# Four reorderings in a two-layer trunk: columns in a shared PSUM bank, three outputs of the layer norm first, ten weight lows on VectorE, four outputs at a time

## The chip, the core and the metric

The kernel runs on one core of a Trainium2 chip. The metric is the device time of that core in microseconds (us). The engines are TensorE (PE in the profile), VectorE (DVE), ScalarE (ACT), GpSimd (POOL) and SyncE (SP). SyncE and GpSimd issue the transfers from HBM (DMA).

## What is computed

A trunk of two layers over 1024 tokens of 1024 channels, all in float32. Each layer has a token mixer and a SwiGLU FFN, each behind an RMS norm and shifted, scaled and gated by a modulation vector. In layer 0 the mixer is a convolution module, in layer 1 a pooling mixer.

```python
def conformer_conv(h, w1, b1, w_dw, b_dw, ln_g, ln_b, w2, b2):
    u = h @ w1 + b1
    a, g = jnp.split(u, 2, axis=-1)
    u = a * jax.nn.sigmoid(g)
    u = lax.conv_general_dilated(u, w_dw[:, None, :], ...) + b_dw   # depthwise, causal, width 31
    u = jax.nn.silu(layer_norm(u, ln_g, ln_b))
    return u @ w2 + b2

def reference(x, c, ...):
    c_act = jax.nn.silu(c)
    for i in range(DEPTH):
        mod = c_act @ ada_w[i] + ada_b[i]
        sh_m, sc_m, g_m, sh_f, sc_f, g_f = jnp.split(mod, N_ADA, axis=-1)
        h = modulate(rms_norm(x, norm_mix_g[i]), sh_m, sc_m)
        y = conformer_conv(h, ...) if i % 2 == 0 else multiscale_pool(h, ...)
        x = x + (1.0 + g_m)[:, None, :] * y
        h = modulate(rms_norm(x, norm_ffn_g[i]), sh_f, sc_f)
        y = (jax.nn.silu(h @ w_gate) * (h @ w_up)) @ w_down
        x = x + (1.0 + g_f)[:, None, :] * y
    return rms_norm(x, final_g)
```

`multiscale_pool` takes trailing means over 2, 4, 8 and 16 tokens in four groups of channels, and then a linear map for each group. The FFN has 2816 inner columns, 22 tiles of 128.

## The kernel before

**Tiles.** The channels lie on the 128 partitions in eight tiles, the tokens in two chunks, A and B, of 512 columns. Nearly all products are 128x512: a weight tile of 128x128, 512 tokens moving. To keep float32 precision every operand is split into a high and a low half, and a product is three matmuls (high by high, high by low, low by high: `products`, L420). A unit of work is mostly one weight tile row of 128x1024, which makes 8 products, 24 matmuls.

**Weights.** `load_weight` (L406 to L418) fetches a weight as `raw` with SyncE, ScalarE rounds it to the high half (a CAST), and the low half comes about in one of two ways. By default, ScalarE writes the rounded negative of the weight into the low tile and GpSimd issues a transfer that adds the weight from HBM onto it (L414): that takes ScalarE a second pass, a place in GpSimd's queue and a second fetch. With `low` given, that engine subtracts the high half from `raw` in one operation. There are nine units of buffer (`W_BUFS`), of which a weight costs two halves, so that few weights are held ahead. `run_units` (L541 to L572) goes through the list of units in order. After each unit and at each weight taken it starts the load of the next weight as long as the held ones fit.

**Order.** TensorE's order is the order in which the program is written; VectorE, ScalarE and GpSimd get the operations as units and tasks emit them, with a running estimate of the engines' clocks that decides where a task takes its next step and which engine does a flexible operation (`either`). Instructions on an engine run in their order, so whatever waits holds what is behind it. Operations of these engines all have the line of the helper, L108; matmuls have L130.

**Convolution stage.** For each tile `p`, TensorE makes `a` and `g`, ScalarE the sigmoid `t<-g` and VectorE the product `u`. The 31 taps are split: VectorE adds its part into `ca`, ScalarE multiplies (`pr`) and GpSimd adds (`pa`); VectorE joins them (`ca<-pa,ca`), makes `u` and adds it to `acc`. The layer norm (`layer_norm_silu`, L777 to L812) starts with the product `mean` of `acc`, then `var` and `rstd`, and then for each of eight tiles SiLU, `vhi` and `vlo`. `conv_out` (L814 to L838) makes the outputs `y`; its first unit makes outputs 0 and 1 together, tile by tile of the layer norm, the others one by one. It is called for A right after the convolution stage, and for B near the end of A's FFN of layer 0.

**Modulation.** `ada_columns` (L360 to L385) runs beside it: `ada` sums for one of the four remaining vectors, loads of two tiles (`adaw`) at a time; ScalarE copies the rows; `columns_done` (L389 to L399) turns the rows into columns by four small matmuls into `adac`, and VectorE adds the bias into `mod`, from which GpSimd makes the `gains`. PSUM has six banks for `mm` tiles, which are handed out in turn: `ada`, `adac`, `a`, `g`, `y`, `gate`, `up` and `dn` all take from them, and a new tile waits for the readers of the old tile in its bank.

**FFN.** `ffn_p1` (L907) makes `gate` and `up` of one inner tile, then `t`, `ghi`, `glo`; `ffn_p2` (L932 to L942) makes the eight outputs `dn` of two or more inner tiles, and after each VectorE updates `x`. `ffn` (L944 to L957) lists them, `ffn_mixed` (L1175 to L1201) does so for the FFNs whose first and last inner tiles are made plainly and whose middle is made for both chunks at once in a scheme of fewer products. At each change of chunk the pooling task of the other chunk (`pool_mixed`, L861) and its windows (`win`) run on VectorE and GpSimd beside the products.

Of the kernel before, what the change touches and what calls it, by code (L numbers as in the profile page):

```python
# [19 lines left out]
KT = D // P  # L20
F = 2816
NF = F // P
# [91 lines left out]
def trunk(ctx, tc, xT, c, vec, ada, adan, w1, w2, wgu, wdn, wpl, wph, out):  # L114
# [131 lines left out]
    def bank(name):  # L246
        return ps.tile([P, 512], F32, tag="mm", name=nm(name))
# [110 lines left out]
    Q = D // 4  # L358

    def ada_columns(js):  # L360


        todo = [(j, k) for j in js for k in range(KT)]
        src = lambda j, k: adan[k, :, (j - 2) * D : (j - 1) * D]
        ws = [ada_load(src(*t)) for t in todo[:ADA_BUFS]]
        rows, done = None, iter(())
        for i, (j, k) in enumerate(todo):
            if i % ADA_BUFS == 0:
                yield "load" if i else "late"
                next(done, None)  # L370
                if rows is not None:
                    done, rows = columns_done(j - 1, rows), None
                    next(done)
            if k == 0:
                acc = bank("ada")
            w = ws.pop(0)
            for g in range(4):
                matmul(acc[32 * g : 32 * g + 32, :Q], ccols[:, k, :], w[:, g * Q : g * Q + Q], start=k == 0, stop=k == KT - 1)
            clock["PE"] -= 1.3
            if i % ADA_BUFS == ADA_BUFS - 1:  # L380
                ws += [ada_load(src(*t)) for t in todo[i + 1 : i + 1 + ADA_BUFS]]
            if k == KT - 1:
                rows = tmp.tile([P, Q], F32, tag="rows", name=nm("rows"), bufs=1)
                S_.copy(rows, acc[:, :Q])
        held_back.append((j, rows))  # L385

    held_back = []

    def columns_done(j, rows):  # L389

        cols = bank("adac")
        for h in range(2):
            matmul(cols[:, 4 * h : 4 * h + 4], rows[:, h * P : h * P + P], quarters, start=True, stop=True)
        yield
        m = mod[:, j * KT : (j + 1) * KT]
        V_.tensor_tensor(m.rearrange("p (q h) -> p q h", h=2), cols[:, :KT].rearrange("p (h q) -> p q h", h=2),
                         V("ada_b", j * KT, KT).rearrange("p (q h) -> p q h", h=2), op=ADD)
        ada_gains(0, j, 0, KT, G_)
        ada_done.add((0, j))  # L399
# [6 lines left out]
    def load_weight(src, n=D, load=nc.sync.dma_start, summed=False, low=None):  # L406
        raw = raws.tile([P, D], F32, tag="raw", name=nm("raw"))[:, :n]
        as_src = lambda t: t if len(src.shape) == 2 else t.rearrange("p (a b) -> p a b", a=src.shape[1])
        load(as_src(raw), src)
        hi, lo = (wts.tile([P, D], F32R, tag="w", name=nm("w"))[:, :n] for _ in range(2))  # L410
        S_.copy(hi, raw)
        if summed:
            S_.activation(lo, raw, AF.Copy, scale=-1.0)
            order(nc.gpsimd.dma_start(as_src(lo), src, accum_op=ADD))  # L414
            clock["G"] = max(clock["G"], clock["PE"]) + 1.0
            return hi, lo
        (low or either(n)).tensor_tensor(lo, raw, hi.bitcast(F32), op=SUB)
        return hi, lo  # L418
# [119 lines left out]
    def unit(emit, *weights):  # L538
        units.append((weights, emit))

    def run_units(cap, early):  # L541

        queue = [w for ws, _ in units for w in ws]
        loaded = list(early)
        del queue[: len(early)]
        used = [0]
        cost = lambda w: 4 if isinstance(w, Pair) else 2

        def ahead():
            held = sum(cost(w) for w in loaded) + used[0] + reserve[0]  # L550
            while queue and (held + cost(queue[0]) <= cap or not loaded or isinstance(queue[0], Pair) and all(
                    isinstance(w, Pair) and w.made is not None for w in loaded)):
                w = queue.pop(0)
                held += cost(w)
                loaded.append(w.load() if isinstance(w, Pair) else load_weight(w, summed=True))
                if len(loaded) > 1:
                    break

        st["ahead"] = ahead
        for ws, emit in units:  # L560
            took = [0]

            def take():
                ahead()
                w = loaded.pop(0)
# [248 lines left out]
    def conv_out(ch, squares, then=None):  # L814

        def done(d, b):
            t = temp(ch.n)
            S_.activation(t, b, AF.Identity, bias=V("conv_b2", d))
            xs = x[ch.i][d]
            V_.scalar_tensor_tensor(xs, t, gate_m[:, d : d + 1], xs, op0=MUL, op1=ADD)  # L820
            squares.add(d)

        def emit_of(ds):
            def emit(take):
                wts = [take() for _ in ds]
                bs = [bank("y") for _ in ds]
                for k in range(KT):
                    for wt, b in zip(wts, bs):
                        products(b, wt, k, st["v", ch.i][k], k == 0, k == KT - 1)
                    if len(ds) > 1:  # L830
                        pace()
                for d, b in zip(ds, bs):
                    done(d, b)
            return emit
        for ds in [(0, 1), *((d,) for d in range(2, KT))]:
            unit(emit_of(ds), *[w2[d] for d in ds])
            if then is not None and len(ds) > 1:
                unit(then)  # L838
# [62 lines left out]
    def update(ch, d, b, gate, l):  # L901

        xs = x[ch.i][d]
        V_.scalar_tensor_tensor(xs, b, gate[:, l * KT + d : l * KT + d + 1], xs, op0=MUL, op1=ADD)
# [27 lines left out]
    def ffn_p2(ch, l, fs, pick):  # L932
        def emit(take):
            wd = [take() for _ in fs]
            gs = [st.pop(("g", ch.i, f)) for f in fs]
            for d in range(KT):
                b = output("dn", pick)
                for i, (g, wt) in enumerate(zip(gs, wd)):
                    products(b, wt, d, g, i == 0, i == len(gs) - 1)
                update(ch, d, b, gate_f, l)  # L940
                pace()
        return emit, tuple(wdn[l, f] for f in fs)  # L942

# [231 lines left out]
    def ffn_mixed(ch, l, until, at_end=False):  # L1175

        before = []
        for f in range(0, PLAIN, 2):
            before += [ffn_p1(ch, l, f, True, False), ffn_p1(ch, l, f + 1, True, False)]
            if f:  # L1180
                before.insert(-1, ffn_p2(ch, l, [f - 2, f - 1], True))
        mates = [Pair(ch, l, f, which) for f in range(PLAIN, until, 2) for which in range(2)]
        mine, theirs = [None] * len(mates), []
        for i, f in enumerate(range(PLAIN - 2, until - 2, 2)):
            first, second = Downs(ch, l, (f, f + 1), (0, 1)), Downs(ch, l, (f, f + 1), (2, 3))
            for at, d in ((2 * i + 1, first), (2 * i + 2, second)):
                if at < len(mates):
                    mine[at] = d
                else:
                    theirs.append(d)  # L1190
        last, = theirs
        before.insert(-1, (lambda take: mine[1].fetch(), ()))
        paired = [(lambda take: mates[0].prepare(), ())]
        for i, me in enumerate(mates):
            if i + 1 == len(mates):
                paired.append((lambda take: reserve.__setitem__(0, 2), ()))
            paired.append(ffn_pair(ch, l, me, mates[i + 1] if i + 1 < len(mates) else None, mine[i], (mine + [last])[i + 1]))
        paired.append((lambda take: last.load(last.dps[1]), ()))
        rest = ffn(ch, l, True, at_end, until, ffn_p2(ch, l, [until - 2, until - 1], True))
        rest[1:1] = [alone(last)]  # L1200
        return before, paired, rest  # L1201

    def ending(ch, l, fs):
# [246 lines left out]
        conv_in((B, p))  # L1450
    need("ln_a")
    sq_a = Squares(A)
    conv_out(A, sq_a, lambda take: [now(columns_done(*g)) for g in held_back])
    unit(lambda take: T.__setitem__("norm_a", Task(norm(A, 0, True, ("h", 0), squares=sq_a), True)))
    for p in rest[len(rest) - HOLD :]:
        conv_in((B, p))
# [138 lines left out]
```

## Time and profile before

| | us |
|---|---|
| three runs | 1815.33, 1812.46, 1815.14 (median 1815.14) |
| profiled execution | 1812.82, its span 1811.0 |
| TensorE busy | 1774.8 (98%), 9748 matmuls |
| VectorE, ScalarE, GpSimd busy | 1304.9 (72%), 1037.7 (57%), 573.0 (32%) |
| read from HBM | 334.73 MB, 187 GB/s over the span |

A row of the profile has the start, the time of one (or of a few alike), the engine, the line, the operation, the tiles (out<-in, buffer numbers left out), and in brackets the idle time before it and what ended it. Matmuls overlap, so that one of 0.39 us starts every 0.23 us or so. `PEclk` is the clock that TensorE was granted, as a share of the full one.

### The profile page before, as it was taken

To read this page: it belongs to the slowest core of one execution; us is meant where nothing else is said; L and a number is where in the kernel's file an instruction comes from. 1 tells how busy PE (TensorE), PEld (TensorE's weight loads), DVE (VectorE), ACT (ScalarE), POOL (GpSimd) and SP (SyncE) were. 2 spreads that over 40 slices of the span, in tenths; PEclk is the share of its full clock that TensorE was granted. 3 is DMA by queue.
4 is the path that set the end of the run, shared out by engine and by line. 5 is a ranking of instruction groups with operands and counts; after the bars stand their busy time and mean duration, and the time that the engine had idled before them with its cause. 6 is when DMAs were issued, how large, how long until landed. Compare 5 with 4: busy or idle time off the path is not lost.

```text
span 1811.0 us, 26241 instructions
## 1 busy us (share of the span) xinstructions
PE 1774.8 (98%) x9748; PEld 1518.9 (84%) x9748; DVE 1304.9 (72%) x2126; ACT 1037.7 (57%) x1607; POOL 573.0 (32%) x627
## 2 busy tenths in 40 slices
PE   9999999999999999999999999999999999999997
PEld 7767777888888887899997878999978889999986
DVE  8689846988774239799977467787694568887745
ACT  4776667766656356555554456555545546555543
POOL 0389624878823112311126122111151221011111
PEclk9999999999999999999999999999999999999998
DMA  9867867889878897976757878555578876655562
GB/s 309 277 182 231 235 170 186 224 217 232 228 192 218 230 224 187 269 195 196 217 145 177 190 167 195 150 129 139 134 167 199 184 160 167 182 140 140 128 141 70
DMA packets 115377, 340.63 MB, mean 188 GB/s; under 512 B 11441, under 2 KB 21809, under 8 KB 115250
## 3 DMA queue, kind: packets, MB, share of 16 engines
q1 hardware_dynamic: 76656, 222.56, 37.0%
q0 software_dynamic: 37440, 115.36, 35.5%
q8 instruction: 76, 1.25, 0.3%
q10 hardware_dynamic: 1154, 1.05, 0.2%
q14 instruction: 51, 0.42, 0.1%
HBM read 334.73 MB, written 4.19 MB: 187 GB/s over the span
## 4 chain that ended last, share of the span: by engine, by line
PE 87%; DVE 5%; DMA 3%; issue 2%; ACT 2%; POOL 2%; POOLq 0%; ACTq 0%
PE gate L130 24%; PE up L130 23%; PE dn L130 23%; PE y L130 5%; PE a L130 3%; PE g L130 3%; PE first L130 2%; DMA w<-in_wdn_dram 1%; DVE t L108 1%; DMA adaw<-in_adan_dram 1%; PE ada L130 1%; DVE win L108 1%; DMA w<-in_wgu_dram 1%; DVE x L108 1%; ACT w L108 1%
## 5 line engine op out<-in xcount | busy, mean ns | idle before, releaser
L130 PE MATMUL dn<-ghi,w 128*128 128x512 f32 (+1 forms) x1440 | 469.0, 388 | 3.1 <-DMA w<-in_wdn_dram 1.7
L108 ACT ACTIVATE w<-raw 128x1024 fp32r<-128x1024 f32 (+1 forms) x260 | 241.0, 927 | 333.0 <-PE dn L130 116.5
L108 ACT CAST w<-raw 128x1024 fp32r<-128x1024 f32 (+1 forms) x390 | 320.0, 823 | 128.6 <-PE up L130 53.3
L108 DVE SCALAR_TENSOR_TENSOR x<-dn,gains,x 128x512 f32<-128x512 f32 (+1 forms) x360 | 262.6, 734 | 80.5 <-PE dn L130 77.3
L130 PEld LDWEIGHTS dn<-ghi,w 128*128 128x128 f32 x1440 | 268.4, 188 | 56.5 <-DMA w<-in_wdn_dram 2.5
L130 PE MATMUL gate<-hhi,w 128*128 128x512 f32 (+1 forms) x1088 | 311.7, 360 | 3.9 <-DMA w<-in_wgu_dram 3.9
L130 PE MATMUL up<-hhi,w 128*128 128x512 f32 (+1 forms) x1088 | 310.1, 358 | 0.0
L130 PE MATMUL dn<-glo,w 128*128 128x512 f32 (+1 forms) x720 | 278.6, 387 | 0.9 <-POOL glo L108 0.9
L108 POOL TENSOR_TENSOR pa<-pa,pr 128x512 f32<-128x512 f32 x170 | 233.7, 1476 | 23.1 <-ACT pr L108 20.5
L130 PEld LDWEIGHTS gate<-hhi,w 128*128 128x128 f32 x1088 | 197.2, 189 | 36.0 <-DMA w<-in_wgu_dram 4.7
L1049 POOL DMA_DIRECT2D w<-in_wgu_dram x80 | 69.8, 872 | 493.4 <-ACT w L108 158.5
L130 PEld LDWEIGHTS up<-hhi,w 128*128 128x128 f32 x1088 | 196.6, 189 | 30.5
L130 PE MATMUL gate<-hlo,w 128*128 128x512 f32 (+1 forms) x544 | 195.6, 360 | 1.4 <-DVE hlo L108 1.4
L130 PE MATMUL up<-hlo,w 128*128 128x512 f32 (+1 forms) x544 | 194.6, 358 | 0.0
L414 POOL DMA_DIRECT2D w<-in_wgu_dram x96 | 86.6, 903 | 318.5 <-ACT w L108 295.2
L108 DVE TENSOR_TENSOR t<-t,up 128x512 f32<-128x512 f32 (+1 forms) x88 | 54.9, 624 | 169.9 <-PE up L130 157.0
L108 DVE SCALAR_TENSOR_TENSOR ca<-u,vecs,ca 128x512 f32<-128x512 f32 x250 | 173.6, 747 | 0.9
L130 PEld LDWEIGHTS dn<-glo,w 128*128 128x128 f32 x720 | 135.8, 189 | 23.9 <-POOL glo L108 1.2
L108 ACT ACTIVATE pr<-u,vecs 128x512 f32<-128x512 f32 x170 | 115.0, 717 | 23.6 <-POOL pa L108 16.6
L130 PEld LDWEIGHTS gate<-hlo,w 128*128 128x128 f32 x544 | 103.0, 189 | 18.2 <-DVE hlo L108 2.3
L108 DVE TENSOR_TENSOR w<-raw,w 128x512 fp32r<-128x512 f32 (+1 forms) x130 | 94.1, 731 | 31.7 <-ACT w L108 28.5
L130 PEld LDWEIGHTS up<-hlo,w 128*128 128x128 f32 x544 | 102.6, 189 | 15.6
(190 smaller groups left out, 3331.5 us busy)
## 6 DMA issues: line engine op xcount, KB each, us to landing
raw<-in_wgu_dram SPq DMA_DIRECT2D x176, 512.0 KB, 4.9
w<-in_wgu_dram POOLq DMA_DIRECT2D x96, 512.0 KB, 8.0
raw<-in_wdn_dram SPq DMA_DIRECT2D x88, 512.0 KB, 5.5
adaw<-in_ada_dram SPq DMA_DIRECT2D x64, 512.0 KB, 5.8
w<-in_wdn_dram POOLq DMA_DIRECT2D x48, 512.0 KB, 8.4
raw<-in_w_dram SPq DMA_DIRECT2D x42, 512.0 KB, 6.7
w<-in_wgu_dram POOLq DMA_DIRECT2D x80, 256.0 KB, 5.5
adaw<-in_adan_dram SPq DMA_DIRECT2D x32, 512.0 KB, 6.2
```

What stands on the lines that cost most here:

```text
L108: self.last = self.order(getattr(self.eng, name)(out, *args, **kw))
L130: last_mm[0] = nc.tensor.matmul(out, lhsT, rhs, start=start, stop=stop, **kw).ins.name
L414: order(nc.gpsimd.dma_start(as_src(lo), src, accum_op=ADD))
L1049: order(nc.gpsimd.dma_start(lo, src, accum_op=ADD))
```

## The change

Four edits, which touch no arithmetic:

1. The columns of a modulation vector (`columns_done`) no longer take a bank of their own (`adac`), but eight columns behind the sums in the `ada` bank of the next vector, which is taken a little earlier. Only the last vector, held back, still has an `adac` bank.
2. `conv_out` makes the outputs 0, 1 and 2 together, then 3 to 7 one by one.
3. `own` marks a unit's weights so that VectorE makes their low half. It is used for the first `ffn_p2` of each `ffn_mixed` and for one `ffn_p1` of the rest in two of the three: ten weights in all, in five pairs.
4. In a plain FFN, the last `ffn_p2` (inner tiles 20 and 21) makes four outputs at a time: first all four from tile 20, then all four from tile 21.

```diff
                 next(done, None)
+                if k == 0:
+                    acc = bank("ada")
                 if rows is not None:
-                    done, rows = columns_done(j - 1, rows), None
+                    done, rows = columns_done(j - 1, rows, acc[:, Q : Q + KT]), None
                     next(done)
-            if k == 0:
-                acc = bank("ada")
...
-    def columns_done(j, rows):
-
-        cols = bank("adac")
+    def columns_done(j, rows, cols):
+
...
+    def own(unit_):
+        return unit_[0], tuple(Own(w) for w in unit_[1])
+
...
-                loaded.append(w.load() if isinstance(w, Pair) else load_weight(w, summed=True))
+                if isinstance(w, Own):
+                    loaded.append(load_weight(w.src, low=V_))
+                else:
+                    loaded.append(w.load() if isinstance(w, Pair) else load_weight(w, summed=True))
...
-        for ds in [(0, 1), *((d,) for d in range(2, KT))]:
+        for ds in [(0, 1, 2), *((d,) for d in range(3, KT))]:
...
-            for d in range(KT):
-                b = output("dn", pick)
+            step_ = 1 if pick or fs[-1] != NF - 1 else 4
+            for d0 in range(0, KT, step_):
+                ds = range(d0, d0 + step_)
+                bs = [output("dn", pick) for _ in ds]
                 for i, (g, wt) in enumerate(zip(gs, wd)):
-                    products(b, wt, d, g, i == 0, i == len(gs) - 1)
-                update(ch, d, b, gate_f, l)
+                    for d, b in zip(ds, bs):
+                        products(b, wt, d, g, i == 0, i == len(gs) - 1)
+                for d, b in zip(ds, bs):
+                    update(ch, d, b, gate_f, l)
                 pace()
...
-                before.insert(-1, ffn_p2(ch, l, [f - 2, f - 1], True))
+                before.insert(-1, own(ffn_p2(ch, l, [f - 2, f - 1], True)))
...
+        if not at_end:
+            rest[4] = own(rest[4])
...
-    conv_out(A, sq_a, lambda take: [now(columns_done(*g)) for g in held_back])
+    conv_out(A, sq_a, lambda take: [now(columns_done(*g, bank("adac"))) for g in held_back])
```

The first place is the end of the convolution stage on GpSimd, before. `pa` collects GpSimd's taps of the last tile, the DMAs add the low halves of three weights of the layer norm's outputs, and the `u<-u,ny` rows follow the mean.

```order
L414 DMA w_1985<-in_w_dram 128x1024
L108 TENSOR_TENSOR pa_1824<-pa_1824,pr_1920 128x512
L108 TENSOR_TENSOR pa_1824<-pa_1824,pr_1939 128x512
L108 TENSOR_TENSOR pa_1824<-pa_1824,pr_1943 128x512
L108 TENSOR_TENSOR pa_1824<-pa_1824,pr_1947 128x512
L108 TENSOR_TENSOR pa_1824<-pa_1824,pr_2022 128x512
L414 DMA w_2123<-in_w_dram 128x1024
L108 TENSOR_SCALAR gains<-mod 128x8
L108 TENSOR_TENSOR gains<-gains,vecs 128x8
L414 DMA w_2134<-in_w_dram 128x1024
L108 TENSOR_TENSOR u_623<-u_623,ny_2069 128x512
```

The same place on GpSimd in the changed program (the numbers of the names are two or three lower there).

```order
L108 TENSOR_TENSOR pa_1822<-pa_1822,pr_1918 128x512
L413 DMA w_2120<-in_w_dram 128x1024
L108 TENSOR_TENSOR pa_1822<-pa_1822,pr_1937 128x512
L108 TENSOR_TENSOR pa_1822<-pa_1822,pr_1941 128x512
L108 TENSOR_TENSOR pa_1822<-pa_1822,pr_1945 128x512
L413 DMA w_2131<-in_w_dram 128x1024
L108 TENSOR_TENSOR pa_1822<-pa_1822,pr_2019 128x512
L108 TENSOR_SCALAR gains<-mod 128x8
L108 TENSOR_TENSOR gains<-gains,vecs 128x8
L108 TENSOR_TENSOR u_623<-u_623,ny_2066 128x512
```

Both of the last two DMAs moved up, the first past four of the adds, the second past the `gains` and the last `pa`.

The second place is the change from chunk B to chunk A between the layers, on GpSimd before: the pooling windows of two tiles (`win`), and the low halves of the weights that the plain `gate` and `up` of inner tile 18 (`in_wgu`) and the next `dn` (`in_wdn`) take.

```order
L108 TENSOR_TENSOR win_9153<-win_9152 128x524
L108 TENSOR_TENSOR win_9152<-win_9153 128x520
L414 DMA w_9187<-in_wgu_dram 128x1024
L108 TENSOR_TENSOR win_9181<-hp_8882 128x526
L108 TENSOR_TENSOR win_9153<-win_9152 128x512
L414 DMA w_9196<-in_wgu_dram 128x1024
L108 TENSOR_TENSOR win_9153<-win_9153,recip 128x15
L108 TENSOR_TENSOR win_9153<-win_9153,hp_8881 128x15
L414 DMA w_9268<-in_wdn_dram 128x1024
```

On VectorE in the changed program the same two low halves stand between the updates of `x` and the pooling's casts and lows (`mxhi`, `mxlo`).

```order
L108 CAST mxhi_9127<-win_9103 128x512
L108 SCALAR_TENSOR_TENSOR x_6_91<-dn_9150,gains,x_6_91 128x512
L108 TENSOR_TENSOR w_9182<-raw_9179,w_9181 128x1024
L108 TENSOR_TENSOR mxlo_9128<-win_9103,mxhi_9127 128x512
L108 SCALAR_TENSOR_TENSOR x_7_92<-dn_9167,gains,x_7_92 128x512
L108 TENSOR_TENSOR w_9190<-raw_9187,w_9189 128x1024
L108 SCALAR_TENSOR_TENSOR win_9148<-win_9148,hp_8876 128x497
L108 TENSOR_TENSOR win_9176<-win_9177 128x520
```

GpSimd keeps none of the two DMAs, and takes the windows of 524 and 512 columns of the last tile in exchange, ahead of the DMA for the next `dn`.

The third place is the start of chunk A's outputs on TensorE in the changed program: three outputs (`y_2303` to `y_2305`), each with the high and low half of its weight, for the first tile of the layer norm, and then the second tile.

```order
L130 MATMUL y_2303<-vhi_2220,w_2119 128x512
L130 MATMUL y_2303<-vlo_2221,w_2119 128x512
L130 MATMUL y_2303<-vhi_2220,w_2120 128x512
L130 MATMUL y_2304<-vhi_2220,w_2130 128x512
L130 MATMUL y_2304<-vlo_2221,w_2130 128x512
L130 MATMUL y_2304<-vhi_2220,w_2131 128x512
L130 MATMUL y_2305<-vhi_2220,w_2281 128x512
L130 MATMUL y_2305<-vlo_2221,w_2281 128x512
L130 MATMUL y_2305<-vhi_2220,w_2282 128x512
L130 MATMUL y_2303<-vhi_2222,w_2119 128x512
```

Before, the second tile of the layer norm came after the first two outputs' six matmuls; now it comes after nine.

More of the change, by code (lines that the diff above doesn't have):

```diff
@@ L539, in unit, with __init__ @@
         units.append((weights, emit))
+    class Own:
+        def __init__(self, src):
+            self.src = src
+    def own(unit_):
+        return unit_[0], tuple(Own(w) for w in unit_[1])
     def run_units(cap, early):
```

## The prediction

> **What bounds the kernel now.** I read the page first, then the waits of TensorE, then the clock by stretches.
>
> ```profile
> PE 1774.8 (98%) x9748; PEld 1518.9 (84%) x9748; DVE 1304.9 (72%) x2126; ACT 1037.7 (57%) x1607; POOL 573.0 (32%) x627
> ```
>
> TensorE is busy 98% of 1811.0 us, and the change takes none of its matmuls away. All it can win is in the 36 us of idle time, and in stretches at a lower clock. So the waits of TensorE tell which idle time the four parts aim at (total, times, longest):
>
> ```profile
> PE a L130 <- ACT t L108: 4.3, 1, 4.3
> PE gate L130 <- DMA w<-in_wgu_dram: 3.9, 2, 2.1
> PE y L130 <- POOL vlo L108: 0.6, 1, 0.6
> PE y L130 <- DVE vlo L108: 0.6, 2, 0.4
> PE y L130 <- ACT vhi L108: 0.5, 2, 0.3
> ```
>
> The one `a` wait is part 1's, the five `y` waits are part 2's, the two `gate` waits part 3's. The stretches after them and the stage after the first wait (columns: busy time and count of each engine, then the granted clock, DMA share, GB/s):
>
> ```profile
> core 0: us, PE busy (x) PEld busy (x) DVE busy (x) ACT busy (x) POOL busy (x), PEclk, DMA share, GB/s
> 120.90:211.60 90.70, 86.45 (x554) 65.71 (x552) 88.20 (x124) 59.64 (x83) 82.74 (x78) 0.96 0.85 237
> 133.00:140.00 7.00, 6.52 (x29) 4.37 (x30) 6.54 (x11) 4.56 (x7) 7.00 (x7) 0.59 0.55 123
> 984.00:990.00 6.00, 6.00 (x20) 4.78 (x21) 2.57 (x5) 0.62 (x1) 1.12 (x2) 0.72 1.06 251
> ```
>
> After a long wait the clock falls: 0.59 over 7 us is 2.9 us of matmuls lost, 0.72 over 6 us is 1.7. In the convolution stage (120.9 to 211.6) VectorE is busy 88.20 of 90.70 us: there it, not TensorE, has nothing to spare.
>
> **Part 1, the modulation columns share a bank.** Before, the column sums took a bank of their own, and the next `a` got the bank of an older `g`, which ScalarE had still to read.
>
> ```profile
> 128.84 0.39 PE L130 MATMUL g<-hhi,w 128*128 128x512 f32 x1
> 133.48 0.79 PE L130 MATMUL a<-hhi,w 128*128 128x512 f32 x1 [4.25 <-ACT t L108]
> 132.74 0.69 ACT L108 ACTIVATE t<-g,vecs 128x512 f32<-128x512 f32 x1 [0.47 <-POOL pa L108]
> ```
>
> The sigmoid `t<-g` ends at 133.43 and `a` starts then. Without the extra bank `a` gets the bank of an `a` that VectorE left long before, and its `g` takes the late bank about 6 us later, when it is free. So 4.25 us and some 2.6 of the lower clock go: TensorE is 6.9 us ahead from there on. What is late next is the layer norm's `mean`:
>
> ```profile
> 205.96 1.30 POOL L108 TENSOR_TENSOR pa<-pa,pr 128x512 f32<-128x512 f32 x1 [0.19 <-ACT pr L108]
> 207.69 0.88 POOL L414 DMA_DIRECT2D w<-in_w_dram  x1 [0.43 <-ACT w L108]
> 208.58 0.70 DVE L108 TENSOR_TENSOR ca<-pa,ca 128x512 f32<-128x512 f32 x1
> 210.16 1.42 DVE L108 TENSOR_TENSOR acc<-acc,u 128x512 f32<-128x512 f32 x2
> 211.69 1.07 PE L130 MATMUL mean<-acc,ones 128*128 128x512 f32 x2
> 211.66 1.06 ACT L108 ACTIVATE w<-raw 128x1024 fp32r<-128x1024 f32 x1 [3.44 <-PE g L130]
> ```
>
> VectorE's last `acc` ends at 211.58, TensorE's last product before `mean` about then too. It is a tie; with TensorE early, VectorE alone sets `mean`, and of its 2.50 idle us in the stage at most that much can go. Besides, GpSimd's order now has the weight transfer whose low ScalarE makes after the last `g` (the row at 211.66, which waits for it) ahead of the last `pa`. From the end of `g`: ScalarE 1.06, hand-overs and the issue about 1.3, `pa` 1.30, then `ca` to the end of `acc` 3.0 (208.58 to 211.58): 6.7 us. TensorE ends `g` near 204.8, so this chain gives 211.5, again a tie. The 6.9 us come back as a wait at `mean`, and that long a wait lowers the clock once more: `mean` (1.07) takes nearly twice as long, and `ada` and `a` behind it lose some, part of it hidden under the waits for the variance. I take +1.5 for this against the 6.9 gained and given back; bounds: −1 (VectorE gains its idle time, the clock costs what it can't hide) and +4 (the 2.9 of the row at 133.00 plus a us on the chain). The shared bank adds an edge too: the next sums on TensorE wait for VectorE's `mod`, which reads the columns beside them. I count nothing for it: where VectorE is behind, TensorE would only wait there for part of what it waits at `mean` anyway.
>
> **Part 2, three outputs first.**
>
> ```profile
> 231.68 0.49 PE L130 MATMUL y<-vhi,w 128*128 128x512 f32 x1
> 246.16 0.50 PE L130 MATMUL adac<-quarters,rows 128*128 128x4 f32 x4
> 245.42 1.06 ACT L108 ACTIVATE w<-raw 128x1024 fp32r<-128x1024 f32 x1 [1.47 <-PE y L130]
> 246.89 0.90 POOL L414 DMA_DIRECT2D w<-in_w_dram  x1 [4.56 <-ACT w L108]
> w<-in_w_dram POOLq DMA_DIRECT2D x3, 512.0 KB, 8.7
> 634.54 1.06 ACT L108 ACTIVATE w<-raw 128x1024 fp32r<-128x1024 f32 x1 [7.68 <-PE y L130]
> 636.00 0.85 POOL L414 DMA_DIRECT2D w<-in_w_dram  x1 [9.32 <-ACT w L108]
> w<-in_w_dram POOLq DMA_DIRECT2D x5, 512.0 KB, 8.3
> 646.52 0.62 PE L130 MATMUL y<-vhi,w 128*128 128x512 f32 x2
> 646.97 0.39 PE L130 MATMUL y<-vlo,w 128*128 128x512 f32 x1
> ```
>
> A matmul follows the last one by 0.227 us (two from 646.52 to 646.97). Chunk A: 48 matmuls would take 10.9 us and took 14.48 (231.68 to 246.16): 3.6 lost, at a pace of 14.48/8 = 1.81 us a step of the layer norm. With three outputs a step is 9 matmuls, 2.04 us, so TensorE is now the slower; some 0.6 us of waits stay at the start. Gain 3.0. But the three hold six weight buffers of nine, and one unit of 24 matmuls (5.45 us) is loaded behind them in place of two. The low half of the second unit behind starts when the triple frees its first buffer (245.42, [<-PE y]), is issued 1.5 us later and lands 7 to 8.7 us after that. The trigger moves 1.7 us later, the landing to 255.5 to 257.3; the unit needs it at about 254.9 (end of the triple 248.65, columns 0.36, 5.45, two matmuls). I take a stall of 1.1: A gives −1.9 (−3.0 to −0.6).
>
> Chunk B had no `y` wait. The same chain: 634.54, issued 636.00, landed 8.0 to 8.3 later (644.2), wanted at 646.97. The trigger moves by 24 matmuls less two, 5.0 us; the landing to 649.2; the demand stays at 646.97. Stall about 2.2, less what a quieter queue saves: I take +1.9 (0 to +3.6, the top if the clock falls as after the 983.89 wait below).
>
> By the Trainium skill's "DMA: Bandwidth & Descriptors", section "Anatomy of one DMA — SWDGE (gpsimd) path", such a transfer takes about 2.0 us and its bytes at 436 GB/s, for 512 KB an estimate of 3.2 us. The rows say 8.3 and 8.7 and decide; by the page neither stall would come and the sum below would be 3 us lower.
>
> **Part 3, ten lows by VectorE.**
>
> ```profile
> 983.89 0.73 PE L130 MATMUL gate<-hhi,w 128*128 128x512 f32 x2 [1.81 <-DMA w<-in_wgu_dram]
> 1354.03 0.72 PE L130 MATMUL gate<-hhi,w 128*128 128x512 f32 x2 [2.06 <-DMA w<-in_wgu_dram]
> 974.31 2.26 POOL L108 TENSOR_TENSOR win<-win 128x524 f32<-128x524 f32 x2 [0.68 <-DVE mxlo L108]
> 976.52 0.87 POOL L414 DMA_DIRECT2D w<-in_wgu_dram  x1
> 975.58 0.74 DVE L108 SCALAR_TENSOR_TENSOR x<-dn,gains,x 128x512 f32<-128x512 f32 x1
> L108 DVE TENSOR_TENSOR w<-raw,w 128x1024 fp32r<-128x1024 f32 x10 | 12.2, 1220 | 3.1 <-ACT w L108 3.0
> ```
>
> The weight of 983.89 lay ready for its transfer while GpSimd waited and added windows; issued at 976.52, it landed with the stall's end, 7.4 us later. Now VectorE makes the low in 1.22 us, behind the update of the seventh output (the row at 975.58), so from about 976.3 to 977.6, and the weight is wanted at 982.1 (983.89 less 1.81). The stall goes (1.81 and hand-over, about 2.0), and with it the lost clock in 984 to 990, of which I count 1.2. The same at 1354.03: 2.2, with no lower clock after it. Against it: two window adds go from VectorE to GpSimd and stand ahead of the next two transfers there, which may cost 0.8. Sum −5.4, bounds −5.9 and −2. The six other lows (three pairs) are 7.3 us of VectorE in places where no matmul waited for a weight; they are covered by VectorE's 28% idle time; without it a pair would hold up the updates, and TensorE for their banks, by up to 2.4 us. I count 0.
>
> The Trainium skill's "TensorE: Matmul & The Clock Gate", section "HAM oscillation — how this bites in real kernels", names idle gaps over about 3.4 us as those that lower the clock. The row 984 to 990 shows 0.72 behind a 1.81 us wait, and decides; by the page the sum would be 1.2 us smaller.
>
> **Part 4, four outputs at a time at the end of layer 0 of A.**
>
> ```profile
> 692.71 0.40 PE L130 MATMUL dn<-ghi,w 128*128 128x512 f32 x1
> 694.09 0.50 PE L130 MATMUL dn<-ghi,w 128*128 128x512 f32 x1 [0.98 <-ACT ghi L108]
> 695.47 0.50 PE L130 MATMUL dn<-glo,w 128*128 128x512 f32 x1 [0.88 <-POOL glo L108]
> 694.12 1.29 POOL L108 TENSOR_TENSOR glo<-t,ghi 128x512 fp32r<-128x512 f32 x1 [0.26 <-ACT ghi L108]
> ```
>
> From start to start the two waits cost 1.38 − 0.227 = 1.15 us each. The first output now does three matmuls of tile 20 (from 692.25) and then needs tile 21. With four outputs twelve come first, 2.7 us, to 694.97: `ghi` (ready at 694.05) is there, `glo` (695.41) is wanted at 695.2. Gain 2.3 − 0.2 = 2.1 (−1 to −2.4). The four banks come free by then, as the updates follow the products.
>
> **Sum.** 1.5 − 1.9 + 1.9 − 5.4 − 2.1 = −6.0 us. The profiled execution took 1812.8 (span 1811.0), the median of the runs is 1815.1, 2.3 above it: 1806.8 by the one, 1809.1 by the other. I predict 1808.
>
> **Rivals.** Forecast (−6, give or take 3): 0.50.
> (a) The 6.9 us of part 1 survive in part: `mean` comes early because VectorE and GpSimd, undisturbed, use up their idle time, and the clock stays up. For it: 2.5 us of idle; against it: VectorE busy 88.20 of 90.70. −2.5 − 7.5 = −10, 1803 by the profiled execution and 1805 by the median: 0.10.
> (b) Slower: GpSimd's last `pa` queues behind the weight transfer that waits for the last `g`. It decides if TensorE does not keep its lead up to there (transfers held it: DMA share 0.85 in the stage). If `g` ends at 211.5 as before, `mean` starts at 218.3: +6.7, and 2.9 for the clock, in place of +1.5: −7.5 + 9.6 = +2.1, 1815 to 1817. The point is `g` ending later than 205; each us later costs one. For it: the order; against it: TensorE's busy 86.45 of 90.70 us leave, beside the 4.25 of the `a` wait, nothing that it waited for there. 0.15.
> (c) Part 3 does not reach its end: VectorE comes to the lows late, behind the casts and windows (1.22 us each, wanted at 982.1), or the weights after them are late on GpSimd. The stall moves on by a unit: −6.0 + 5.4 = −0.6, 1812 to 1814: 0.13.
> (d) Transfers land soon enough after the triples, as the queue is emptier: −6 − 3 = −9, 1804 to 1806; for it: queueing behind each other may be part of the 8.7; against it: the 8.3 and 8.7. The Trainium skill's page "DMA: Bandwidth & Descriptors", as cited above, would have it so. 0.12.
>
> **Range and chances.** A difference under 0.2%, 3.6 us, can't be told from none. The range goes from (a) with (d) on top, 1800, into (b), 1816. Faster: 0.40 of the forecast's 0.50, all of (a) and (d): 0.62. Same: the rest of the forecast, (c), some of (b): 0.28. Slower: 0.10, the upper part of (b).
>
> **What would show it.** No `a` wait near 129, `mean` still at 211 to 212 but now with 5 to 7 us of wait for `acc`, and a lower clock behind it; `y` of A in about 17 us for three outputs; a wait for a transfer at the fifth `y` of both chunks; no `gate` waits near 980 and 1350; the two `dn` waits near 694 down to 0.2. I am wrong in part 1 if `mean` moves by over 3 us either way against the start of the stage, in part 2 if B shows no wait, in part 3 if a wait for a weight stands near 980.

## The result, and the profile after

The change made the kernel slower. Twelve runs after it took 1820.39 us in the median (1815.01 to 1829.26), twelve before it 1813.9 (1810.7 to 1816.23): a ratio of 1.0036 (95% interval 1.0022 to 1.0050). The forecast of 1808, within 1800 to 1816, was wrong in its sign. The profiled execution after the change took 1815.8 us, one of the fastest of the twelve; its span is 1814.0, 3.0 longer than before. So what follows places 3.0 us matmul by matmul; that a median run loses 6.5 was seen only through the runs of single parts below.

The waits of TensorE after the change (total, times, longest):

```profile
PE mean L130 <- DVE mod L108: 7.0, 1, 7.0
PE dn L130 <- DMA w<-in_wdn_dram: 5.2, 4, 1.9
PE ada L130 <- DMA adaw<-in_adan_dram: 4.2, 3, 2.6
PE y L130 <- DMA w<-in_w_dram: 2.2, 3, 1.3
```

Every wait that the change aimed at is gone: no `a` wait for ScalarE (4.3 before), no `gate` wait for a weight (3.9 before), no `dn` wait for `ghi` or `glo`, no `y` wait for `vhi` or `vlo`. Each has an heir: `mean`, `dn` for the next weights, `ada`, and `y` for a weight. Put beside each other, the starts of the same matmuls on the two timelines show where time was won and lost:

| matmul | before | after | after less before |
|---|---|---|---|
| the `a` that waited for its bank | 133.48 | 129.27 | −4.2 |
| `mean` of A's layer norm | 211.69 | 214.33 | +2.6 |
| first `y` of A | 231.68 | 237.03 | +5.4 |
| sixth `y` of A | 263.43 | 266.74 | +3.3 |
| fifth `y` of B, its weight's low half | 646.52 | 652.03 | +5.5 |
| last `dn` of those made four at a time | 705.43 | 709.11 | +3.7 |
| `gate` that waited at 983.89 | 983.89 | 985.31 | +1.4 |
| `dn` of the next unit | 997.23 | 998.54 | +1.3 |
| `gate` that waited at 1354.03 | 1354.03 | 1353.11 | −0.9 |
| the fourth `dn` of the unit behind it | 1368.75 | 1371.45 | +2.7 |

Part 1 goes from −4.2 to +5.4 by the first `y`. Here is why, on TensorE, GpSimd, ScalarE and VectorE around `mean`:

```profile
206.92 0.39 PE L130 MATMUL g<-hhi,w 128*128 128x512 f32 x1
214.33 2.05 PE L130 MATMUL mean<-acc,ones 128*128 128x512 f32 x2 [7.02 <-DVE mod L108]
...
196.44 7.55 POOL L108 TENSOR_TENSOR pa<-pa,pr 128x512 f32<-128x512 f32 x5
203.94 0.87 POOL L413 DMA_DIRECT2D w<-in_w_dram  x1
204.55 4.32 POOL L108 TENSOR_TENSOR pa<-pa,pr 128x512 f32<-128x512 f32 x3
208.97 0.88 POOL L413 DMA_DIRECT2D w<-in_w_dram  x1
209.58 1.57 POOL L108 TENSOR_TENSOR pa<-pa,pr 128x512 f32<-128x512 f32 x1
...
207.52 1.04 ACT L108 ACTIVATE w<-raw 128x1024 fp32r<-128x1024 f32 x1
...
211.18 0.69 DVE L108 TENSOR_TENSOR ca<-pa,ca 128x512 f32<-128x512 f32 x1 [1.66 <-POOL pa L108]
```

The last `pa` starts at 209.58, behind two transfers, and ends at 211.15; before it ended at 207.26. VectorE waits 1.66 us for it, so that GpSimd, not VectorE, sets `mean`. (The row of `mean` names `mod`, which VectorE makes in 0.16 us right behind the last `acc`.) TensorE waits 7.02 us, and then (clock in the last column but two):

```profile
214.30:221.00 6.70, 6.67 (x31) 3.63 (x32) 3.87 (x7) 3.65 (x7) 3.63 (x5) 0.75 0.42 121
```

The clock over these 6.7 us is 0.75, and the two products of `mean` at their start take 2.05 us in place of 1.07. A later transfer for `ada` is late as well and costs 2.62 at 234.78 (0.9 was the longest such wait before).

### The profile page after: what moved, and what is told of

Same layout as the page of the kernel before. It is cut to its first block, busy times and chain, and to the rows that moved or that the text cites. A ratio compares the mean times of both kernels' runs of the same rounds, so it can differ in the third digit from the quotient of the medians.

```text
span 1814.0 us, 26209 instructions
## 1 busy us (share of the span) xinstructions
PE 1774.6 (98%) x9748; PEld 1518.4 (84%) x9748; DVE 1317.4 (73%) x2133; ACT 1028.3 (57%) x1597; POOL 568.6 (31%) x620
## 4 chain that ended last, share of the span: by engine, by line
PE 83%; DMA 4%; DVE 4%; issue 4%; POOL 3%; ACT 2%; POOLq 0%; SPq 0%; DVEq 0%; ACTq 0%
PE dn L130 23%; PE gate L130 23%; PE up L130 22%; PE y L130 4%; PE a L130 3%; PE first L130 2%; DMA w<-in_wdn_dram 2%; PE g L130 2%; DMA adaw<-in_adan_dram 1%; ACT w L108 1%; POOL pa L108 1%; DMA w<-in_w_dram 1%; PE ada L130 1%; POOL w L413 1%; DVE t L108 1%
## 5 line engine op out<-in xcount | busy, mean ns | idle before, releaser
L108 ACT ACTIVATE w<-raw 128x1024 fp32r<-128x1024 f32 (+1 forms) x250 | 230.4, 921 | 304.0 <-PE dn L130 100.7
L1064 POOL DMA_DIRECT2D w<-in_wgu_dram x80 | 69.7, 871 | 499.4 <-PE up L130 147.5
L413 POOL DMA_DIRECT2D w<-in_wgu_dram x92 | 82.2, 893 | 312.8 <-ACT w L108 289.1
L108 DVE TENSOR_TENSOR w<-raw,w 128x512 fp32r<-128x512 f32 (+1 forms) x140 | 107.7, 775 | 33.0 <-ACT w L108 29.7
```

The costliest lines, as they stand in the source:

```text
L108: self.last = self.order(getattr(self.eng, name)(out, *args, **kw))
L1064: order(nc.gpsimd.dma_start(lo, src, accum_op=ADD))
```

## The experiments

Ratios are to the kernel before, from runs on the same chip, with a 95% interval.

**Each part alone: part 1** (ratio 1.0021, 1.0012 to 1.0030; median 1817.8 against 1814.1).

```diff
-                    done, rows = columns_done(j - 1, rows), None
+                    done, rows = columns_done(j - 1, rows, acc[:, Q : Q + KT]), None
...
-        cols = bank("adac")
```

> Part 1 alone. Theory (from the trace after the change): TensorE gains 4 to 7 us at the old wait near 129 and loses more at mean, because GpSimd's order puts a weight transfer ahead of the last pa: mean starts near 214.3, 2.6 us later than before (211.7), with a wait of about 7 us, a lower clock behind it and a longer wait for adaw near 235. Sum +4 to +6 us. Rival A (the prediction as it stood): mean near 211.5, sum +1.5 us. Rival B: the loss at mean belongs to another part, and part 1 alone gains 2 us or more.

In its trace `mean` starts at 214.29, behind 6.63 us of wait. The theory held, its sum but for a little: part 1 alone costs 3.7 us (+4 to +6 was expected), and is as late at `mean` as the whole change.

**Part 2 alone** (1.0035, 1.0022 to 1.0049; 1819.25).

```diff
-        for ds in [(0, 1), *((d,) for d in range(2, KT))]:
+        for ds in [(0, 1, 2), *((d,) for d in range(3, KT))]:
```

> Part 2 alone. Theory: chunk A gains 2 to 3 us less about 1 at the fifth output, chunk B loses 2 us in waits for the weights' low halves, sum -1 to +1 us. Rival: the transfers land soon enough when nothing else is changed, no wait in B, sum -3 us.

Slower than either theory had it. Its three waits for a weight, on TensorE:

```profile
256.96 0.73 PE L130 MATMUL y<-vhi,w 128*128 128x512 f32 x2 [1.59 <-DMA w<-in_w_dram]
...
626.10 0.73 PE L130 MATMUL y<-vhi,w 128*128 128x512 f32 x2 [0.75 <-DMA w<-in_w_dram]
...
649.02 0.73 PE L130 MATMUL y<-vhi,w 128*128 128x512 f32 x2 [2.22 <-DMA w<-in_w_dram]
```

The first is A's fifth output (1.1 was forecast), the last B's fifth (2.2 by the working, 1.9 taken). The one at 626.10 was not forecast: the third output of the triple needs its weight's low half 9.5 us earlier than before (635.64), and it had just not landed. Beside the same matmuls before, TensorE is 2.8 us ahead up to the first of these waits; from the second wait to behind the third it loses 5.2 us, 1.6 of them at a lower clock behind the third.

**Part 3 alone** (1.0003, 0.9994 to 1.0012; 1814.9).

```diff
-                before.insert(-1, ffn_p2(ch, l, [f - 2, f - 1], True))
+                before.insert(-1, own(ffn_p2(ch, l, [f - 2, f - 1], True)))
...
+        if not at_end:
+            rest[4] = own(rest[4])
```

> Part 3 alone. Theory: both gate waits (983.9 and 1354.0) go, -2 us each, but the next weights with a transfer on GpSimd (dn, near 997 and 1366) land late instead, and one of the new waits lowers the clock: sum -2 to +1 us. Rival (the prediction): no new wait of over 0.8 us, sum -5.4 us.

No gain, as the theory had it: 7.6 us of `dn` waits for transfers stand where 3.9 of `gate` and 1.7 of `dn` waits stood. GpSimd at the first of the two places, before it the wait on TensorE, and last the page's wait:

```profile
996.25 0.73 PE L130 MATMUL dn<-ghi,w 128*128 128x512 f32 x2 [2.45 <-DMA w<-in_wdn_dram]
...
973.89 4.49 POOL L108 TENSOR_TENSOR win<-win 128x524 f32<-128x524 f32 x3 [0.68 <-DVE mxlo L108]
...
984.85 0.89 POOL L414 DMA_DIRECT2D w<-in_wdn_dram  x1
986.78 0.87 POOL L414 DMA_DIRECT2D w<-in_wdn_dram  x1 [0.36 <-issue]
...
PE dn L130 <- DMA w<-in_wdn_dram: 7.6, 5, 2.5
```

Before, GpSimd issued these two at 981.83 and 984.30 (the first stood ahead of the last windows). Now the windows stand ahead, three in a row of 4.49 us, and the first transfer leaves 3.0 us later, though TensorE is 2 us earlier. The `gate` wait of 1.81 became a `dn` wait of 2.45.

**Part 4 alone** (1.0012, 1.0004 to 1.0021; 1815.43).

```diff
+            step_ = 1 if pick or fs[-1] != NF - 1 else 4
```

> Part 4 alone. Theory and prediction agree: the two dn waits near 694 shrink from 1.15 us each to 0.2 together, sum -2.1 us (-1 to -2.4). Rival: the updates of four outputs come at once, a bank is late, sum 0.

At the place itself the forecast was exact: the last `dn` of the unit starts at 703.40 in place of 705.43, 2.0 us earlier. At 764 the gain is gone: `gate` waits for a bank that ScalarE reads late. In the waits of TensorE, and then on SyncE's queue, VectorE and again SyncE before the change:

```profile
PE gate L130 <- ACT t L108: 3.7, 1, 3.7
```

```profile
747.79 4.78 SPq L140 DMA_DIRECT2D adaw<-in_ada_dram  x2
752.66 0.44 SPq L1007 DMA_DIRECT2D raw<-in_wgu_dram  x1
...
750.99 1.22 DVE L108 SCALAR_TENSOR_TENSOR adaw<-adaw,cact 128x1024 f32<-128x1024 f32 x1
```

```profile
743.96 5.82 SPq L140 DMA_DIRECT2D adaw<-in_ada_dram  x2
750.68 1.37 SPq L1003 DMA_DIRECT2D raw<-in_wgu_dram  x2
```

SyncE can load the next `adaw` only when VectorE has reduced the one before (750.99 to 752.21), and the `raw` of the pair's weights stands behind it. With four outputs between two calls of the planner, VectorE's order is another from the edit up to some 825 us, and that reduction comes later. The raw leaves 2.0 us later while TensorE is 2.0 earlier, and ScalarE's first cast of it starts at 761.47 in place of 757.77.

**Part 1 with two transfers behind the taps**, those of the weights of outputs 0 and 1 (1.0020, 1.0011 to 1.0029; 1817.13).

```diff
+            if id(src) in late:
+                tc.add_manual_dep(d.ins, late["pa"], edge, reason="behind the taps")
```

> Part 1 with the two weight transfers behind the last pa in GpSimd's order (nothing else moved). Theory 1 (GpSimd's queue sets mean): the last pa ends 1.2 to 1.6 us earlier, mean starts near 213.0 instead of 214.3; what is left of the lateness is GpSimd's earlier waits for weight lows (5.5 us in five places against 3.6 in two before), so it does not come back to 211.7. The two weights land later, which costs nothing unless y waits. Sum +2 to +3 us against before, 1.3 us less than part 1 alone. Theory 2 (VectorE alone sets mean, as the prediction had it): mean stays near 214.3. Rival: the weights now land late and y waits, no gain.

GpSimd and TensorE in that run:

```profile
200.44 8.53 POOL L108 TENSOR_TENSOR pa<-pa,pr 128x512 f32<-128x512 f32 x6
208.91 1.76 POOL L415 DMA_DIRECT2D w<-in_w_dram  x2
...
212.15 2.04 PE L130 MATMUL mean<-acc,ones 128*128 128x512 f32 x2 [6.00 <-DVE mod L108]
```

`mean` comes 2.1 us earlier than in part 1 alone; GpSimd's queue is shown as what held it. Of the 2.1, the transfers are 1.4, as the theory had it: the last nine adds take from 195.56 to 208.97 here, and from 196.26 to 211.11 with the two transfers among them. The other 0.7 GpSimd had won before that, which the edit does not explain. But TensorE still waits 6.00 us, has the lower clock behind that (2.04 for `mean`) and a 2.3 us wait for `adaw`, and the whole is still 3.4 us slower than before. Part 1 alone lost 3.7: the earlier `mean` does not show in the time, where 1.3 us were expected.

**Part 3 with the next unit's lows too** (0.9962, 0.9950 to 0.9974; 1807.92 against 1813.78).

```diff
             rest[4] = own(rest[4])
+            rest[5] = own(rest[5])
```

> Part 3 with the lows of the next unit's two weights (the dn that waited at 997 and 1366) by VectorE too, four lows more. Theory: the gate waits stay away and the dn waits that took their place go, sum -4 to -5 us against before. Rival: the wait moves on to the next weight whose low GpSimd transfers, or VectorE's 1.2 us operations hold up the updates, sum -1 to +1 us as for part 3 alone.

The theory held, and the gain is larger than it said: 5.9 us. The four lows more take GpSimd's queue out of the way of TensorE at both places, and of 7.6 us of `dn` waits this is left:

```profile
PE dn L130 <- DMA w<-in_wdn_dram: 0.9, 1, 0.9
```

**Part 4 with the planner called as often as before** (0.9993, 0.9984 to 1.0002; 1812.55).

```diff
                         products(b, wt, d, g, i == 0, i == len(gs) - 1)
+                        if step_ == 4 and (d - d0) % 2 and not (i and d - d0 == 3):
+                            pace()
```

> Part 4 with the planner called after every two half outputs, as often as before the change, instead of once after four outputs: the products are in the same order, VectorE's order downstream is another. Theory 1 (order): the 3.7 us wait of gate at 764 came from an adaw reduction that stood later in VectorE's order, behind which SyncE's adaw load and the raw load of the pair queue; with the reductions earlier again the wait is below 1 us and the gain of 2.0 us stays, sum -1 to -2 us. Theory 2 (transfers are the bound near 750, DMA share about 1): the wait stays at 3 us or more whatever the order, sum 0 to +2.

The `gate` wait shrank to 1.0 (its row: the same group, once), with the raw issued at 751.06 instead of 752.66, and the median is 1.2 us below that of the kernel before, where part 4 alone was 1.3 above it. The interval takes in no change; it does not meet that of part 4 alone. So the order on VectorE made most of that wait. The theory's sum is only half there: of 1.8 us won near 695, the trace has 0.4 left behind this wait.

```profile
746.18 4.78 SPq L140 DMA_DIRECT2D adaw<-in_ada_dram  x2
751.06 0.93 SPq L1009 DMA_DIRECT2D raw<-in_wgu_dram  x2
```

**Part 2 with five lows by VectorE** (0.9989, 0.9981 to 0.9998; 1812.16).

```diff
-            unit(emit_of(ds), *[w2[d] for d in ds])
+            unit(emit_of(ds), *[Own(w2[d]) if d in ((4, 5), (2, 4, 5))[ch.i] else w2[d] for d in ds])
```

> Part 2 with five lows by VectorE instead of the adding transfer: outputs 4 and 5 of A, 2, 4 and 5 of B. Theory (release, ScalarE, GpSimd's transfer, landing is the chain that is too long for one unit): the y waits for a weight (4.6 us in part 2 alone) go to below 1 us, A keeps its 3 us, sum -2 to -3 us against before. Rival: the first fetch of the weight (raw) is late as well, or VectorE's order puts the lows late; y still waits 2 us or more, sum 0 to +3.

No `y` waits for a weight any more in its trace, and chunk A keeps 2.4 us (its fourth output starts at 249.70 in place of 252.10). Each taken against the kernel before on its chip, that is 6.7 us better than part 2 alone. The chain from a buffer's release over ScalarE and GpSimd to the landing was the cause.

**All three mended, without part 1** (0.9941, 0.9927 to 0.9954; 1802.42 against 1814.01).

```diff
+            rest[4] = own(rest[4])
+            rest[5] = own(rest[5])
...
+        for ds in [(0, 1, 2), *((d,) for d in range(3, KT))]:
+            unit(emit_of(ds), *[Own(w2[d]) if d in ((4, 5), (2, 4, 5))[ch.i] else w2[d] for d in ds])
...
+                        if step_ == 4 and (d - d0) % 2 and not (i and d - d0 == 3):
+                            pace()
```

> Parts 2 to 4 in their mended form (three outputs first with five lows by VectorE, the ten lows and the four after them by VectorE, four outputs at a time with the planner called as often as before), without part 1. Theory: the gains lie in different stages and add: -6.9 - 1.9 - 1.3 = -9 to -11 us against before, about 1804. Rival: a lead won early is lost at the next stage that transfers set, so that the sum is no better than the fourteen lows alone, -7.

They add to 11.6 us, more than 5.9, 1.6 and 1.2 one by one: this is the fastest version of the study, and beats both kernels.

**The change without part 1** (1.0019, 1.0009 to 1.0029; 1816.69).

```diff
-                    done, rows = columns_done(j - 1, rows, acc[:, Q : Q + KT]), None
+                    done, rows = columns_done(j - 1, rows), None
```

> The change without part 1 (parts 2, 3 and 4 as they were made). Theory: part 1 costs the whole change what it cost alone, 3.7 us by the medians and 5.4 in its trace, so that this takes 1815 to 1817, +1 to +3 us against before. Rival: parts 1 and 2 share their loss (both wait for the same weights around 235 to 260), then this is within 1.5 us of the whole change, 1819 to 1821.

2.7 us above the kernel before, where the whole change is 6.5 above it. The 3.8 between are what part 1 costs alone, though the two intervals overlap.

**Six taps left out, before and with part 1** (one run each: 1836.12 and 1821.24). These tell nothing.

```diff
-            self.next, self.acc, self.part, self.busy = 0, None, None, 0
+            self.next, self.acc, self.part, self.busy = 6 * (ch.i == 0), None, None, 0
```

> The kernel before, which leaves out six of the 31 taps of each channel tile of chunk A (less work for VectorE and GpSimd in the convolution stage). Theory: with the layer norm's sums no longer late, mean still starts at 211 to 212, as TensorE's own 211.69 with the 4.25 us wait for the bank sets it. Rival: mean was set by VectorE, and moves earlier by 3 us or more.

> Part 1 alone with the same six taps left out. Theory: what part 1 wins for TensorE (4.2 to 5 us at 203) is lost only because VectorE and GpSimd are not done at mean; with less work for them mean starts near 207 and the gain of 4 to 5 us stays beyond it. Rival: mean still waits for 3 us or more (GpSimd's queue behind the weights' lows, or the sums of the modulation), mean at 210 or later.

Since the tasks of the taps were done sooner, the planner put `mean` ahead of two tiles' products, and in both runs another product waits 7 us for VectorE (`ph`). Nothing follows from the two times. The next pair keeps TensorE's order.

**Half the columns in the last taps, before** (0.9999, 0.9987 to 1.0011) **and with part 1** (1.0001, 0.9989 to 1.0013).

```diff
+                    elif low:
+                        V_.scalar_tensor_tensor(self.acc[:, :256], src[:, :256], w(j), self.acc[:, :256], op0=MUL, op1=ADD)
...
+                        G_.tensor_tensor(self.part[:, :256], self.part[:, :256], pr[:, :256], op=ADD)
```

> The kernel before, with the middle taps of chunk A's last two tapped channel tiles made on half their columns (it leaves out the other half; the order of the instructions stays the same on TensorE and all but the same on GpSimd). Theory (mean was a tie): mean stays within 1 us of 211.7, as TensorE's own products end there. Rival (VectorE set it): mean moves earlier by 3 us or more.

> Part 1 with the same half taps. Theory: the wait at mean is below 2 us, mean starts near 207, 4 to 5 us earlier than in the kernel before, there is no lower clock behind it, and 3 us or more of that are left at the end. Rival 1: mean still waits 4 us or more, for GpSimd's queue or the sums. Rival 2: mean is early but the gain is lost in the wait for adaw near 230 (transfers are the bound), less than 1.5 us left at y.

VectorE and TensorE without part 1:

```profile
204.77 1.42 DVE L108 TENSOR_TENSOR acc<-acc,u 128x512 f32<-128x512 f32 x2
...
212.11 1.02 PE L130 MATMUL mean<-acc,ones 128*128 128x512 f32 x2
```

The sums are ready at 206.2, 5.4 us earlier, and `mean` does not move: the kernel before was a tie there, as the prediction said. With part 1 the wait at `mean` is gone, the clock behind it is 1.00, and still `mean` starts at 211.62. TensorE had lost its lead 28 us earlier. Its row, then SyncE's queue ahead of it, in this run and in part 1 alone:

```profile
183.62 1.08 PE L130 MATMUL ada<-adaw,ccols 128*32 128x256 f32 x8 [3.44 <-DMA adaw<-in_adan_dram]
...
171.91 0.33 SPq L140 DMA_DIRECT2D adaw<-in_adan_dram  x1
172.33 0.38 SPq L408 DMA_DIRECT2D raw<-in_w_dram  x1
172.80 7.77 SPq L140 DMA_DIRECT2D adaw<-in_adan_dram  x2
```

```profile
172.08 0.83 SPq L140 DMA_DIRECT2D adaw<-in_adan_dram  x2
172.97 0.54 SPq L408 DMA_DIRECT2D raw<-in_w_dram  x1
```

An `adaw` came 3.44 us late, and the clock behind it is 0.53 up to 187 us. So a transfer took the lead, as rival 2 had it, but at another place. It is not the same program on SyncE, though: here the `raw` of a weight stands between the two `adaw` loads, in part 1 alone behind both, and there no `ada` waits near 180. So the pair shows that the kernel before was a tie of TensorE's products with the sums, and that with early taps the wait at `mean` goes. Whether part 1 would keep its lead if the taps were early and the loads came in the order of part 1 alone stays open.

**The mended parts with part 1 and late transfers** (0.9959, 0.9945 to 0.9973; 1806.9 against 1815.04).

```diff
+                    done, rows = columns_done(j - 1, rows, acc[:, Q : Q + KT]), None
...
+                tc.add_manual_dep(d.ins, late["pa"], edge, reason="behind the taps")
```

> Parts 2 to 4 mended and part 1 with the two transfers behind the last pa. Theory: part 1 still loses 2 to 3.5 us to mean and what follows, 1804.5 to 1806. Rival: with fewer adding transfers around it part 1 gains, 1801 or less.

8.1 us below the kernel before, where the same version without part 1 is 11.6 below it. So part 1 seems to cost some 3.5 us here too, with 5.5 us of wait at `mean`; the two intervals overlap.

## Why the prediction was wrong, point by point

**Part 1: the bank wait.** Right: 4.25 us and the lower clock went, TensorE was ahead by up to 6.6. Right too that the kernel before was a tie at `mean`, and that the gain comes back as a wait there. Wrong is the step "TensorE ends `g` near 204.8, so this chain gives 211.5, again a tie". TensorE ended `g` at 207.3 (a wait of 1.47 us for an `adaw` at 134.19 and smaller ones took the difference), so that the chain of the prediction, 6.7 us, gives 214.0; measured 214.33. That is the outcome of rival (b), which had 0.15, and which named the point ("`g` ending later than 205; each us later costs one").

That the chain fits so well is partly luck, for it was not the last to arrive. ScalarE has the weight ready for its transfer at 208.56, while GpSimd, with no wait since 196.44, is still adding until 208.87. With an earlier `g`, GpSimd's own queue would have held `mean` nearly as long. The prediction looked at that queue only from `g` on. GpSimd's last `pa` ends 3.9 us later than before: the two transfers ahead of it cost 1.4 us in the run that moved them, and further up GpSimd waits 5.8 us in five places for weights from ScalarE, 3.5 in two before. The shared bank, for which the prediction counted nothing, cost nothing that the trace shows: no `ada` waits for VectorE.

Mis-sized is the term of +1.5 behind `mean`, with a bound of +4. The clock and the next `adaw` wait take 2.7 us from `mean` to the first `y`, which with the 2.6 at `mean` makes +5.4. By the medians part 1 costs 3.7. The sign that the prediction set for part 1, a `mean` moved by over 3 us, did not come: it moved 2.6.

**Part 2: A.** The gain of 3.0 was right, and so was a wait for a late low half behind it (in part 2 alone 1.59 at the fifth output, in the whole change 0.61 at the sixth): 5.4 to 3.3 in the table is −2.1, forecast −1.9. **B.** +2.2 in the trace against +1.9, but that is luck. The wait at the fifth output, 2.2 by the working, is only 0.34 in the whole change. Missed is that the third output of the triple itself needs its low half sooner, and that wait is 1.27 (at 631.00). In part 2 alone both waits and the lower clock cost B 5.2 us, beyond the range's end of +3.6. Rival (d) fell: the transfers did not land sooner. There the Trainium skill's "DMA: Bandwidth & Descriptors", section "Anatomy of one DMA — SWDGE (gpsimd) path", is not borne out by these runs: the estimate of 3.2 us from its figures would have left no wait, and there were 1.59 and 2.22 in part 2 alone.

```profile
631.00 0.73 PE L130 MATMUL y<-vhi,w 128*128 128x512 f32 x2 [1.27 <-DMA w<-in_w_dram]
```

**Part 3.** Right: both stalls go, 2.3 and 2.2 us in the table. Wrong is the term "two window adds go from VectorE to GpSimd and stand ahead of the next two transfers there, which may cost 0.8". It is not even in the sum: 2.0, 1.2 and 2.2 make the 5.4 without it. It took nearly the whole gain back: 1.48 and 1.94 us of waits for the next `dn` weights, the second with a lower clock behind it: from 1354.03 to 1368.75 the table loses 3.6.

```profile
998.54 0.73 PE L130 MATMUL dn<-ghi,w 128*128 128x512 f32 x2 [1.48 <-DMA w<-in_wdn_dram]
...
1366.78 0.73 PE L130 MATMUL dn<-ghi,w 128*128 128x512 f32 x2 [1.94 <-DMA w<-in_wdn_dram]
```

The price was read from when the windows used to run, not from when VectorE, with two lows more to do, would let GpSimd run them. In the chain "VectorE, window, transfer, landing" two engines got later at once: the two lows took VectorE 1.41 and 1.64 us there, not 1.22, and the three windows GpSimd 4.49. Rival (c) had this end of it, at 0.13. The sign set for part 3, a wait for a weight near 980, did not come either; the wait stood 15 us further on.

**Part 4.** The size was right (−1.8 in the whole change, −2.0 alone, −2.1 forecast). The mistake was to take the rest of the program as unmoved: in the part alone the new order on VectorE downstream cost more than the gain. In the whole change the raw leaves at 754.36, as late as TensorE is there (3.7 us), and that wait is absent.

**The sum.** By the trace 5.4 − 2.1 + 2.2 − 1.8 − 0.7 = +3.0, where −6.0 was forecast; 3.9 of the 9.0 between are part 1, 4.7 part 3. The medians of the four parts alone add to 3.7 + 5.1 + 0.8 + 1.3 = 10.9, more than the 6.5 of the whole, perhaps since waits that follow each other hide one another; no run shows it. Rivals (b) and (c) both came true in part, and the prediction has no chance for the two together; its terms for them would make −7.5 + 9.6 + 5.4 = +7.5. Why a median run of the whole is 3.5 us worse than the profiled execution's difference is not settled: in the traces at hand the same waits stand with more or less of lower clock behind them.

## What to carry to other kernels

A wait that is removed is worth only what the next bound of the same stage leaves; look for a second and a third engine that end at the same time before counting it, and take away work from those to see. When work is moved to another engine in a kernel with in-order queues, follow the next transfer that queues behind what the engine drops in exchange, and mend that with it: the same idea went from no gain to 5.9 us with four lows more. An edit that calls a planner more or less often changes the order far behind it, so a local gain must be looked for again some stages later.

## What the runs showed of the hardware that was not expected

A wait's length alone does not tell whether the clock falls behind it. Behind the 1.81 us at 983.89 in the kernel before it was 0.72; behind the 2.06 us at 1354.03 in the same execution 1.00, and in part 2 alone, where the wait there was 3.3 us and takes up half of the stretch, 0.72 (clock in the last column but two; 0.52 in the 3 us from 1357, behind the wait):

```profile
1354.00:1360.00 6.00, 5.97 (x26) 4.95 (x27) 1.45 (x3) 1.42 (x2) 0.86 (x1) 1.00 1.05 251
```

```profile
1354.00:1360.00 6.00, 2.95 (x7) 2.37 (x8) 3.10 (x5) 1.80 (x3) 0.86 (x1) 0.72 1.04 227
```

The Trainium skill's "TensorE: Matmul & The Clock Gate", section "HAM oscillation — how this bites in real kernels", speaks of gaps over some 3.4 us. The 1.81 us with 0.72 behind it says that a much shorter one can lower it too; which ones do, these runs do not tell.
